# Joining the first two runs of decay levels in the last head of a gated-linear-attention layer

## The chip, the cores and the metric

The kernel runs on one core of a Trainium2 chip. The metric is device time in microseconds, taken as the median of several runs; the profile is that of one execution. Four compute engines work beside each other: TensorE (PE in the profile), VectorE (DVE), ScalarE (ACT) and GpSimd (POOL). SyncE (SP) issues the transfers between main memory and the core's working memory. TensorE writes only into accumulators (PSUM), which the other engines empty.

## The reference, cut to what matters

The program is a decoder of two layers over 1024 tokens with 1024 features. The first is gated linear attention with four heads, the second a dilated sliding-window attention with eight query heads. Each ends in an output projection, a residual and a layer norm. The change lies in the first layer. There, for every chunk, the reference computes an attention matrix whose products decay with the distance of the two tokens, separately for each of the 128 key features:

```python
b_all = jnp.cumsum(to_chunks(log_a), axis=3)
def step(state, inp):
    qc, kc, vc, bc = inp
    o_inter = jnp.einsum('bhcd,bhde->bhce', qc * jnp.exp(bc), state)
    diff = bc[:, :, :, None, :] - bc[:, :, None, :, :]
    decay = jnp.where(causal, jnp.exp(jnp.where(causal, diff, 0.0)), 0.0)
    att = jnp.einsum('bhid,bhjd,bhijd->bhij', qc, kc, decay)
    o_intra = jnp.einsum('bhij,bhje->bhie', att, vc)
    b_last = bc[:, :, -1:, :]
    new_state = jnp.exp(b_last[:, :, 0, :])[..., None] * state + \
        jnp.einsum('bhcd,bhce->bhde', kc * jnp.exp(b_last - bc), vc)
    return new_state, o_inter + o_intra
```

The head's output is normalised, multiplied by a gate, projected and added to the residual stream.

## The kernel before

**Decay by levels.** The kernel uses chunks of 128 tokens, eight of them. The factor `decay` depends on both tokens and on the feature, so the matrix is not one matmul. The function `levels` (from line 899) splits each 128 x 128 triangle into blocks: for L = 64, 32, 16, 8, 4, 2, 1 the block in which the query lies in the upper and the key in the lower half of a stretch of 2L tokens. Relative to the last token of the lower half both exponents have the right sign, so one tile X of 128 features x 1024 tokens holds the decayed queries in its upper halves and the decayed keys in its lower halves. X takes two subtractions, one exponential and two products (lines 908 to 916). The diagonal needs no decay; it is called L = 0 and uses q and k directly. There are three buffers for X, shared with a later tile `ke`.

**Runs.** The levels are walked in the order 0, 64, 32, 16, 8, 4, 2, 1 (line 904) and collected in the list `pair`. Once it is long enough (line 924), an accumulator tile `lv` of 128 x 512 is taken for every two levels, all their small matmuls (32 columns of the array each, 32 or 64 columns of data) are recorded as one group, and the results are copied out: L = 64 and 32 straight into the attention matrix `AT`, the others through a predicated copy into a compact tile `Dg`, which goes into `AT` behind the last run (line 961). There are two `lv` buffers. One level of 32 columns takes 32 matmuls (level 32 takes 16, level 64 takes 16 of 64 columns), each recorded as two instructions in the profile, as full-precision matmuls are.

In heads 0 to 2 the levels 0, 64, 32 and 16 form one run over both `lv` buffers, and 8 and 4, then 2 and 1, one run each. In head 3, the last, there are four runs of two levels each.

**What surrounds it.** `layer_a` ends with a loop over the heads (lines 1040 to 1050): gate, levels, `state_prep` (decayed queries and keys, with a transpose of the keys on TensorE), projections recorded behind them, and then `chunks` for each half of the tokens, which reads `AT` in its first matmul. For head 3 the projections are its own v and gate (lines 871 and 876), followed by `after`, which loads the stored outputs of the earlier heads for the output projection `out_ln`. The projections' wide matmuls are independent of the levels and fill TensorE while the other engines make the tiles X. Each wide product is done as three matmuls over split numbers (a high and a low part); the names `wh`, `wl`, `xh`, `xl`, `ogh`, `ogl` are these parts.

**Order of the work.** Nothing is issued as it is written. `Sched` records every operation, and `order` (from line 254) plans all of them from start to end with a table of costs: at each step it takes the operation that can begin earliest, and among equals the one recorded first, and for operations open to several engines (`vp`, `va`, `vap`) it also picks the engine. Every engine then executes its instructions in this order. A group is placed as a whole: all its inputs and all its new buffers must be at hand. The planner has no entry for the cost of changing from wide to narrow matmuls. Because all instructions are issued in one place, the profile shows the same line, 452, for nearly all of them; tiles' names tell them apart.

Of the kernel before, what the change touches and what calls it, by code (L numbers as in the profile page):

```python
# [18 lines left out]
GH = 4  # L19
# [578 lines left out]
def trunk(tc, xT, wP, wA, wA12, wAv3, w2, wO, wK, wV0, wV12, wB, wOB, par_d,  # L598
# [126 lines left out]
    def layer_a(t2, t1, after):  # L725
# [15 lines left out]
        def xtile(dt, name, shape=(128, T)):  # L741
            return t1.tile(list(shape), dt, name=name, tag="X", bufs=3)
# [156 lines left out]
        def levels(h):  # L899
            q, k, b = H[h]["q"], H[h]["k"], H[h]["b"]  # L900
            AT, Dg = ATs[h % 2], Dgs[h % 2]
            pair = []

            for li in (NLEV - 1, *range(NLEV - 1)):
                if li < len(LEVELS):
                    L = LEVELS[li]
                    n = T // (2 * L)
                    X = xtile(F32, "X")
                    view = lambda t: t.rearrange("p (n s l) -> p n s l", s=2, l=L)
                    bv, Xv = view(b), view(X)  # L910
                    ref = bv[:, :, 0, L - 1:L].to_broadcast([128, n, L])
                    S.vector.tensor_sub(Xv[:, :, 1, :], bv[:, :, 1, :], ref)
                    S.vp.tensor_sub(Xv[:, :, 0, :], ref, bv[:, :, 0, :])
                    S.scalar.activation(X, X, AF.Exp, scale=1.0 / 16.0)
                    S.vector.tensor_mul(Xv[:, :, 1, :], Xv[:, :, 1, :], view(q)[:, :, 1, :])
                    S.vp.tensor_mul(Xv[:, :, 0, :], Xv[:, :, 0, :], view(k)[:, :, 0, :])
                    lt, rt = X, X
                else:
                    L = 0
                    lt, rt = k, q  # L920


                pair.append((li, L, lt, rt))
                if len(pair) < (4 if h < GH - 1 and L in (0, 64, 32, 16) else 2):
                    continue
                pbs = [ps.tile([128, 2, 256], F32, name="lv", bufs=2) for _ in pair[::2]]
                with S.group():
                    for j, (_, L, lt, rt) in enumerate(pair):
                        pb, i = pbs[j // 2], j % 2
                        for c in range(NCH):  # L930
                            o = c * 128
                            if L == 64:

                                for s in (0, 32):
                                    d = c % 2 * 64 + s
                                    S.tensor.matmul(pb[d:d + 32, i, c // 2 * 64:c // 2 * 64 + 64],
                                                     lt[:, o + s:o + s + 32], rt[:, o + 64:o + 128],
                                                     start=True, stop=True)
                                continue
                            for s in (0, 64) if L == 32 else range(0, 128, 32):  # L940
                                e = s + 32 if L == 32 else s
                                S.tensor.matmul(pb[s:s + 32, i, c * 32:c * 32 + 32], lt[:, o + s:o + s + 32],
                                                 rt[:, o + e:o + e + 32], start=True, stop=True)
                for j, (lj, L, _, _) in enumerate(pair):
                    pb, i = pbs[j // 2], j % 2
                    if L == 64:
                        pl = pb[:, i].rearrange("p (c q) -> p c q", q=64)
                        AP = AT.rearrange("p (c two) i -> p two c i", two=2)
                        for x in range(2):
                            S.va.copy(AP[0:64, x, :, 64:128], pl[x * 64:x * 64 + 64])  # L950
                        continue
                    pl = pb[:, i].rearrange("p (c q) -> p c q", q=32)
                    if L == 32:
                        for s in (0, 64):
                            S.va.copy(AT[s:s + 32, :, s + 32:s + 64], pl[s:s + 32])
                    else:
                        S.vector.copy_predicated(
                            Dg, lmask[:, lj - 2:lj - 1, :].to_broadcast([128, NCH, 32]), pl)
                pair = []
            for s in range(0, 128, 32):  # L960
                S.va.copy(AT[s:s + 32, :, s:s + 32], Dg[s:s + 32])
# [78 lines left out]
        for h in range(GH):  # L1040
            gate(h)
            levels(h)
            state_prep(h)
            for f in ('qg', 'qVg', 'qg', 'vge')[h]:
                {"g": lambda: proj_g(h), "q": lambda: proj_qk(h + 1), "V": proj_v12, "v": lambda: proj_v(3), "e": lambda: after(0)}[f]()
            for g in range(2):
                chunks(h, g)
                finish(h, g)
                if h == GH - 1 and g == 0:
                    after(1)  # L1050
# [632 lines left out]
```

## Time and profile before

| | |
|---|---|
| median of 3 runs | 1153.51 us (1153.29 to 1153.53) |
| profiled execution, its own time | 1154.09 us |
| profiled execution, span from first to last instruction | 1152.2 us |
| granted TensorE clock, mean | 0.998 |
| TensorE busy | 1142.6 us (99%) |
| VectorE, ScalarE, GpSimd busy | 812.5, 457.7, 197.4 us |

The span is shorter than the execution's time, since that also holds what lies before the first and behind the last instruction. A row of the timeline gives start and length in microseconds, engine, line, operation, output and inputs by tile name, shape and count. Times count from the span's start. The four heads of the first layer lie at about 57 to 350 us, the first output projection behind them until about 440, the second layer until about 1100, and the last output projection up to the end.

### The profile page before, as it was taken

The numbers are of one execution on the slowest core, as the hardware profiler recorded it, in microseconds if no ns is written. First come the engines' busy times: TensorE is split into PE (matmuls) and PEld (weight loads), VectorE is DVE, ScalarE is ACT, GpSimd is POOL, SyncE is SP. The second block draws the span as 40 slices with busy tenths as digits, with TensorE's granted clock in tenths as the row PEclk, the third lists the DMA queues.
The fourth block names the chain that finished last, engine by engine and source line by source line (L and its number), as shares of the span: only waits on it lengthen the run. The fifth ranks groups of instructions, "written<-read, shape, count | busy, mean of one in ns | idle before, by whom it ended". The sixth has DMA issues, their size and how long they took to land.

```text
span 1152.2 us, 19793 instructions
## 1 busy us (share of the span) xinstructions
PE 1142.6 (99%) x7780; PEld 975.0 (85%) x7780; DVE 812.5 (71%) x1638; ACT 457.7 (40%) x964; POOL 197.4 (17%) x156
## 2 busy tenths in 40 slices
PE   9999999999999999999999999999999999999997
PEld 9888888889988888888888888888888888888886
DVE  6286862686966699765366868676778778768678
ACT  5355431645463335311214343434323433434342
POOL 1000100112011120221020314131221223213000
PEclk9999999999999999999999999999999999999999
DMA  8111222111144465543611211111151011134545
GB/s 271 56 39 38 74 75 92 38 57 54 59 171 139 139 203 160 173 143 104 210 40 36 56 38 57 38 40 54 38 166 39 20 39 38 39 93 129 188 141 183
DMA packets 93372, 108.39 MB, mean 94 GB/s; under 512 B 43648, under 2 KB 61952, under 8 KB 93280
## 3 DMA queue, kind: packets, MB, share of 16 engines
q1 hardware_dynamic: 93280, 107.13, 29.8%
q8 instruction: 61, 1.00, 0.4%
q14 instruction: 31, 0.25, 0.1%
HBM read 85.94 MB, written 21.17 MB: 93 GB/s over the span
## 4 chain that ended last, share of the span: by engine, by line
PE 94%; DVE 3%; DMA 1%; ACT 1%; issue 0%; SPq 0%; POOL 0%; DVEq 0%; ACTq 0%
PE acc L452 63%; PE lv L452 10%; PE po L452 9%; PE vac L452 7%; PE ms L452 4%; PE pro L452 2%; DVE rt L452 1%; DMA ogf<-ogB 1%; DVE wl L452 1%; DMA xf<-in_xT 0%; DVE x1l L452 0%; ACT wh L452 0%; ACT ogh L452 0%; DVE lnA L452 0%; SPq L452 0%
## 5 line engine op out<-in xcount | busy, mean ns | idle before, releaser
L452 PE MATMUL acc<-x1h,wh 128*128 128x512 f32 x608 | 252.2, 415 | 0.0
L452 PE MATMUL acc<-x1h,wl 128*128 128x512 f32 x608 | 237.6, 391 | 0.0
L452 PE MATMUL acc<-x1l,wh 128*128 128x512 f32 x608 | 237.0, 390 | 0.0
L452 ACT ACTIVATE wh<-wf 128x1024 fp32r<-128x1024 f32 (+2 forms) x104 | 108.1, 1040 | 267.0 <-PE acc L452 168.7
L452 POOL TENSOR_TENSOR wl<-wf,wh 128x1024 fp32r<-128x1024 f32 x41 | 98.3, 2397 | 530.4 <-ACT wh L452 352.3
L452 PEld LDWEIGHTS acc<-x1h,wl 128*128 128x128 f32 x608 | 114.1, 188 | 24.7
L452 PEld LDWEIGHTS acc<-x1l,wh 128*128 128x128 f32 x608 | 114.5, 188 | 21.3
L452 PEld LDWEIGHTS acc<-x1h,wh 128*128 128x128 f32 x608 | 114.4, 188 | 21.0
L452 ACT ACTIVATE P<-P,sts 128x128 f32<-128x128 f32 (+2 forms) x192 | 81.4, 425 | 121.7 <-DVE sts L452 121.4
L452 DVE TENSOR_TENSOR wl<-wf,wh 128x1024 fp32r<-128x1024 f32 (+2 forms) x64 | 80.9, 1265 | 57.3 <-ACT wh L452 45.3
L452 PE MATMUL acc<-xh,wh 128*128 128x512 f32 x256 | 101.7, 397 | 0.0
L452 PE MATMUL acc<-xh,wl 128*128 128x512 f32 x256 | 99.8, 390 | 0.0
L452 PE MATMUL acc<-xl,wh 128*128 128x512 f32 x256 | 99.8, 390 | 0.0
L452 DVE TENSOR_TENSOR t<-acc,cosT 128x512 f32<-128x512 f32 x60 | 41.3, 689 | 65.4 <-PE acc L452 65.3
L452 DVE TENSOR_TENSOR t<-acc,sinT 64x512 f32<-64x512 f32 x120 | 82.6, 688 | 1.6
L452 PE MATMUL lv<-K,Q 128*64 128x64 f32 (+2 forms) x512 | 69.4, 286 | 0.0
L452 DVE CUSTOM_DVE_ANT_0 P<-lv,bmask 128x256 f32<-128x256 f32 (+1 forms) x128 | 46.3, 379 | 29.3 <-PE lv L452 28.5
L452 DVE TENSOR_TENSOR Q<-t,t 128x512 f32<-128x512 f32 x44 | 61.7, 1402 | 1.2
L452 PEld LDWEIGHTS lv<-K,Q 128*128 128x128 f32 (+1 forms) x512 | 53.2, 163 | 10.0 <-issue 1.1
L452 PE MATMUL acc<-ogh,wh 128*128 128x512 f32 x152 | 60.3, 397 | 0.0
L452 PE MATMUL acc<-ogh,wl 128*128 128x512 f32 x152 | 59.2, 390 | 0.0
L452 PE MATMUL acc<-ogl,wh 128*128 128x512 f32 x152 | 59.2, 389 | 0.0
(250 smaller groups left out, 2230.1 us busy)
## 6 DMA issues: line engine op xcount, KB each, us to landing
wf<-in_wB SPq DMA_DIRECT2D x32, 512.0 KB
wf<-in_wA SPq DMA_DIRECT2D x24, 512.0 KB
wf<-in_wO SPq DMA_DIRECT2D x16, 512.0 KB
wf<-in_wOB SPq DMA_DIRECT2D x16, 512.0 KB
wf<-in_wV SPq DMA_DIRECT2D x12, 512.0 KB
res<-in_xT SPq DMA_DIRECT2D x16, 256.0 KB
x1d<-rt SPq DMA_DIRECT2D x16, 256.0 KB
out<-rt SPq DMA_DIRECT2D x16, 256.0 KB
```

Of the source, the lines that this page charges most:

```text
L452: getattr(handle[o.eng], meth)(*[conv(a) for a in args], **{k: conv(v) for k, v in kw.items()})
```

## The change

The condition that ends a run loses its exception for the last head, so that head 3 too collects the levels 0, 64, 32 and 16 into one run, which uses both `lv` buffers and needs three tiles X at once. Its runs of levels 8 and 4, and 2 and 1, stay. No instruction is added or removed; the planner works out the order anew for the whole program.

```diff
@@ -921,7 +921,7 @@
                 pair.append((li, L, lt, rt))
-                if len(pair) < (4 if h < GH - 1 and L in (0, 64, 32, 16) else 2):
+                if len(pair) < (4 if L in (0, 64, 32, 16) else 2):
                     continue
                 pbs = [ps.tile([128, 2, 256], F32, name="lv", bufs=2) for _ in pair[::2]]
```

## The prediction

> **What bounds the kernel now.** I read the page of the profile first, then the busy times by stage, then the order of instructions on each engine around the last head's levels.
>
> ```profile
> span 1152.2 us, 19793 instructions
> PE 1142.6 (99%) x7780; PEld 975.0 (85%) x7780; DVE 812.5 (71%) x1638; ACT 457.7 (40%) x964; POOL 197.4 (17%) x156
> PE 94%; DVE 3%; DMA 1%; ACT 1%; issue 0%; SPq 0%; POOL 0%; DVEq 0%; ACTq 0%
> ```
>
> TensorE (PE) is busy for 99% of the span, and 94% of the chain that ended last lies on it. Busy time alone does not prove the bound, because matmuls are pipelined and their ends are modelled. So I look at the stages (columns: length, then busy time and instructions of each engine, granted clock, DMA share, GB/s):
>
> ```profile
> 285.00:320.00 35.00, 35.00 (x651) 31.82 (x650) 32.01 (x50) 16.69 (x23) 3.79 (x3) 1.00 0.18 62
> 320.00:350.00 30.00, 30.00 (x167) 26.10 (x165) 19.05 (x34) 20.27 (x31) 6.20 (x4) 1.00 0.48 164
> 640.00:1100.00 460.00, 459.46 (x2610) 393.36 (x2609) 340.53 (x896) 175.43 (x534) 112.46 (x102) 1.00 0.25 69
> 1100.00:1152.00 52.00, 45.02 (x221) 37.91 (x219) 44.35 (x75) 20.19 (x34) 1.29 (x1) 0.96 0.45 149
> ```
>
> The changed work lies between 285 and 320. There PE has no idle time at the full clock, and VectorE (DVE) is the next engine at 32.01 of 35 us, so 91%. Only behind 1100 does PE stand still for long (52.00 - 45.02 = 6.98 us). The view of waits names no engine that PE's matmuls waited for in the changed stretch. What decides is therefore PE time, and the order in which DVE serves PE only if something becomes later than PE's other work can cover.
>
> **The two runs that are joined.** The order of PE's instructions in head 3 (start, length, output and inputs, tile, count) shows run one (k·q and level 64), then run two (levels 32 and 16):
>
> ```profile
> 290.47 0.63 PE L452 MATMUL ms<-sq,onesr 128*128 128x512 f32 x2
> 291.03 0.73 PE L452 MATMUL lv<-q,k 128*32 128x32 f32 x62
> ...
> 292.18 0.38 PE L452 MATMUL acc<-wh,xh 128*128 128x256 f32 x1
> 292.40 0.28 PE L452 MATMUL acc<-wl,xh 128*128 128x256 f32 x1
> 292.52 0.28 PE L452 MATMUL acc<-wh,xl 128*128 128x256 f32 x1
> ...
> 300.07 0.28 PE L452 MATMUL acc<-wh,xl 128*128 128x256 f32 x1
> 300.28 1.27 PE L452 MATMUL lv<-X 128*32 128x32 f32 x96
> 301.48 0.39 PE L452 MATMUL acc<-wh,xh 128*128 128x256 f32 x1
> 301.70 0.28 PE L452 MATMUL acc<-wl,xh 128*128 128x256 f32 x1
> ```
>
> In head 2 the same four levels already stand as one run:
>
> ```profile
> 239.42 0.39 PE L452 MATMUL acc<-xl,wh 128*128 128x512 f32 x1
> 239.65 0.39 PE L452 MATMUL acc<-xh,wl 128*128 128x512 f32 x1
> 239.97 0.73 PE L452 MATMUL lv<-q,k 128*32 128x32 f32 x62
> ...
> 240.55 1.67 PE L452 MATMUL lv<-X 128*32 128x64 f32 x126
> 242.14 0.50 PE L452 MATMUL acc<-xh,wh 128*128 128x512 f32 x1
> 242.48 0.40 PE L452 MATMUL acc<-xl,wh 128*128 128x512 f32 x1
> ```
>
> I charge a run with the time from the start of the last foreign matmul before it to the start of the second one behind it, less the steps which those foreign matmuls take anyway: 0.12 us for 256 columns (292.40 to 292.52) and 0.23 us for 512 (239.42 to 239.65). Run two: 301.70 - 300.07 = 1.63, less 2 x 0.12, makes 1.39 us. Run one: 292.40 - 290.47 = 1.93, less 2 x 0.23 and 0.12, makes 1.35 us. The joined run: 242.48 - 239.65 = 2.83, less 2 x 0.23, makes 2.37 us. **The saving is 1.35 + 1.39 - 2.37 = 0.37 us.** About 0.2 us of it is one switch from wide matmuls to narrow ones and back (for run two 301.70 - 300.07 = 1.63 less the 1.20 us from 300.28 to 301.48 and 0.24 leaves 0.19). The runs alone, without their switches, give the lower bound: (292.18 - 291.03) + (301.48 - 300.28) - (242.14 - 239.97) = 1.15 + 1.20 - 2.17 = 0.18 us. I take 0.37, since a switch delays all that stands behind it on a full PE, and keep 0.18 for the range.
>
> **The number of other instructions** does not change: the same 192 level matmuls, the same scratch tiles, two predicated copies and four plain copies out of the accumulators, the same two `lv` buffers. No DMA is added or moved, so nothing on the DMA queue is priced.
>
> **What becomes later.** The joined run needs the scratch tiles X of levels 64, 32 and 16 at once, which are all three that exist. Level 64's tile was free after run one (about 292) and served level 8 from 297.11 on; now it comes free after the joined run. The rows of DVE, ACT and PE that show what this moves:
>
> ```profile
> 297.11 0.68 DVE L452 TENSOR_TENSOR X<-b 128x512 f32<-128x512 f32 x1
> 298.91 0.68 DVE L452 TENSOR_TENSOR X<-b 128x512 f32<-128x512 f32 x1
> 299.63 1.06 ACT L452 ACTIVATE X<-X 128x1024 f32<-128x1024 f32 x1 [0.65 <-DVE X L452]
> 302.00 0.45 DVE L452 COPY_PREDICATED Dg<-lmask,lv 128x256 f32<-128x256 uint8 x1 [1.07 <-ACT AT L452]
> 321.13 1.70 ACT L452 ACTIVATE AT<-Dg 32x256 f32<-32x256 f32 x4
> 325.96 0.69 DVE L452 COPY sg<-acc 128x512 f32<-128x512 f32 x1 [4.86 <-PE acc L452]
> 331.20 0.61 PE L452 MATMUL po<-AT,v 128*128 128x128 f32 x4
> ```
>
> Level 8's two subtractions (0.68 each) and its exponential (1.06) move behind the joined run, together with one predicated copy (0.45): 2 x 0.68 + 1.06 + 0.45 = 2.87 us of work in a chain that had them done early. DVE's idle 1.07 us ahead of 302.00 takes some back, so I expect the third run 1 to 3 us later than 309.81. The other heads give the same from outside (chain of waits; start, length, what):
>
> ```profile
> 135.36 2.18 PE lv L452 x159
> 147.96 1.29 PE lv L452 x98
> 155.62 1.29 PE lv L452 x98
> 240.03 2.18 PE lv L452 x159
> 252.63 1.29 PE lv L452 x98
> 261.68 1.29 PE lv L452 x98
> 309.81 1.30 PE lv L452 x98
> 318.13 1.29 PE lv L452 x98
> ```
>
> From joined run to third run they need 12.60 us (240.03 to 252.63, 135.36 to 147.96), and to the last run 9.05 or 7.66 more. With a joined run at 300.3 this puts the third run at 312.9 and the last at 320.6 to 322.0, so 2 to 4 us later than 318.13.
>
> **I cost this delay at nothing.** What is late next is the attention matrix AT. It is complete at 321.13 + 1.70 = 322.83, but its first reader is the matmul at 331.20, behind the gate projection, whose whole work lies ahead of it on PE in any case. That is a cover of 8.37 us against 2 to 4, and DVE has 4.86 us idle ahead of 325.96 to catch up. If the cover were gone, PE would wait one microsecond per microsecond. From below, an earlier run could gain nothing either, since that PE work stays in front. So the bounds of this term are 0 and, with the whole 2.87 us exposed, +2.9.
>
> **The sum**: the profiled execution took 1154.09 us (span 1152.2, and 1.9 around it). 1154.09 - 0.37 = 1153.72. That execution lies 0.58 above the median of the timed runs, 1153.51, so the forecast for the median is 1153.51 - 0.37 = **1153.1 us**, with 1152.9 to 1156.0 as the bounds of the two terms (the upper with 0.18 saved and 2.9 exposed). What a measurement can tell from no change is about 0.2%, 2.3 us, so this is "no change".
>
> **The rivals.** *The order further on changes for the worse.* The order of all later work is worked out by a planner from start to end, so a shifted DVE queue near 300 can alter it. The price is extra switches on PE at 0.2 us. To be over 0.2% slower it takes (2.3 + 0.37) / 0.2 = 13 of them. With two more in each of the eight query heads of layer B: 1153.1 + 16 x 0.2 = **1156.3**. For it speaks that DVE is 91% busy where the shift occurs. Against it, PE's work up to 331.20 is the same set either way, so the queues can fall back into the old order behind it; and layer B runs in a strict rhythm, which does not look sensitive to how it was entered:
>
> ```profile
> 652.13 2.07 PE acc L452 x9
> 713.09 2.07 PE acc L452 x9
> 774.05 2.07 PE acc L452 x9
> ```
>
> These are the same place in three heads in a row, 60.96 us apart each time. Chance 0.09.
>
> *The levels end too late.* Place: the PE queue at 331.20. It decides from a delay of 8.37 us on; to cost over 0.2% net it needs 8.37 + 2.67 = 11.0 us, and with 12 it gives 1153.1 + 3.6 = **1156.7**. For it: three tiles are held at once, on an engine at 91%. Against: the other heads' spacing allows 4. Chance 0.03. [...]
>
> *The order further on changes for the better.* With two switches fewer in each of eight heads, or half of the 6.98 us won at the end: 1153.1 - 3.2 = **1149.9** or 1149.6. For it: the last stage is the only one where PE stands still, and its order follows from what came before. Against: no part of the change touches it. Chance 0.08.
>
> **How the numbers follow.** The likeliest case, no change within 0.2%, has 0.80, and 1153.1 is its time. Faster by over 0.2% has 0.08, slower 0.12 (0.09 and 0.03). The range is 1151.2 to 1156.3: below it reaches to the edge of 0.2%, above to the first slower case, beyond the exposed delay of 1156.0.
>
> **What would show it.** In the profile after: one run of 192 level matmuls in head 3 at 298 to 301, with about 2.2 us from its start to the next wide matmul; level 8's subtractions behind it; the third run at 311 to 313, the last at 319 to 322; the first matmul on AT within 0.5 us of 331, with no wait on PE ahead of it; layer B with 60.96 us between heads and the same stage times. I am wrong if PE idles before 331, if the stages of layer B change their length by more than 1 us in all, or if the time moves by over 2.3 us.

## The result, and the profile after

The changed kernel took 1157.86 us in the median (six executions, 1156.17 to 1159.83), the kernel before on the same chip 1153.52 (six, 1153.29 to 1155.06). The ratio is 1.0031 with a 95% interval of 1.0021 to 1.0041: **slower by 0.31%**, where 1153.1 us had been forecast. The profiled execution of the changed kernel took 1156.17 us, with these lines on its page:

```profile
span 1154.4 us, 19793 instructions
...
PE 1143.0 (99%) x7780; PEld 974.7 (84%) x7780; DVE 816.2 (71%) x1640; ACT 456.5 (40%) x963; POOL 194.3 (17%) x155
...
q8 instruction: 61, 1.00, 0.4%
...
PE 96%; DVE 3%; issue 1%; ACT 0%; DVEq 0%
```

The counts of PE are those of before; one instruction has gone from ACT and one from POOL to DVE. The busy times by stage, columns as before:

```profile
285.00:320.00 35.00, 33.07 (x604) 30.17 (x606) 29.24 (x48) 15.44 (x23) 2.80 (x2) 1.00 0.18 62
640.00:1100.00 460.00, 460.00 (x2614) 393.98 (x2613) 342.65 (x906) 174.61 (x534) 111.03 (x102) 1.00 0.24 68
1100.00:1154.00 54.00, 47.04 (x229) 39.22 (x227) 44.76 (x76) 21.05 (x34) 1.29 (x1) 0.98 0.44 153
331.00:362.00 31.00, 30.64 (x163) 25.65 (x162) 25.59 (x37) 19.79 (x29) 9.73 (x6) 1.00 0.42 149
```

In the changed stretch PE now stands still for 35.00 - 33.07 = 1.93 us, where it had no idle time. Layer B (640 to 1100) and the end (6.96 us idle against 6.98) are as they were. From 331 to 362 PE executes 163 matmuls where the kernel before executes 169:

```profile
331.00:362.00 31.00, 31.00 (x169) 26.86 (x168) 24.50 (x39) 19.94 (x28) 10.30 (x6) 1.00 0.35 118
```

I matched the matmuls of the two profiled executions by their position in the order of starts (both have 7780) and took the difference of their starts, after less before. It is -0.67 us up to 285, before anything differs; two executions of one same kernel differ there by 0.3 us too (before_mid96 and before_mid96_b, below). It becomes +1.07 by 303, +1.19 by 330 and +2.44 by 362, and stays so to 1050. **So the change costs 1.74 us between 285 and 303, 1.25 us between 331 and 362, and 0.12 us between these two places.** At the end 0.4 us comes back. The two losses have different causes. These sizes are those of the profiled execution, the fastest of the six; the other five have no trace.

### The profile page after: what moved, and what is told of

Its sections match the earlier page's. It is cut to its first block, busy times and chain, and to the rows that moved or that the text cites. A ratio compares the mean times of both kernels' runs of the same rounds, so it can differ in the third digit from the quotient of the medians.

```text
span 1154.4 us, 19793 instructions
## 1 busy us (share of the span) xinstructions
PE 1143.0 (99%) x7780; PEld 974.7 (84%) x7780; DVE 816.2 (71%) x1640; ACT 456.5 (40%) x963; POOL 194.3 (17%) x155
## 4 chain that ended last, share of the span: by engine, by line
PE 96%; DVE 3%; issue 1%; ACT 0%; DVEq 0%
PE acc L452 64%; PE lv L452 10%; PE po L452 9%; PE vac L452 7%; PE ms L452 4%; PE pro L452 2%; DVE rt L452 1%; DVE wl L452 1%; DVE x1l L452 0%; DVE lnA L452 0%; ACT wh L452 0%; DVE oT L452 0%; ACT sq L452 0%; DVE sum L452 0%; DVE ogl L452 0%
## 5 line engine op out<-in xcount | busy, mean ns | idle before, releaser
L452 POOL TENSOR_TENSOR wl<-wf,wh 128x1024 fp32r<-128x1024 f32 x40 | 95.8, 2396 | 513.1 <-ACT wh L452 355.3
```

What stands on the lines that cost most here:

```text
L452: getattr(handle[o.eng], meth)(*[conv(a) for a in args], **{k: conv(v) for k, v in kw.items()})
```

## First loss: PE runs out of instructions

The order of PE's instructions in head 3, after (a bracket names the idle time ahead of a row and what ended it; "issue" is time in which nothing that the profile shows was waited for):

```profile
298.03 0.28 PE L452 MATMUL acc<-wh,xl 128*128 128x256 f32 x1
298.24 0.73 PE L452 MATMUL lv<-q,k 128*32 128x32 f32 x62
...
298.82 1.56 PE L452 MATMUL lv<-X 128*32 128x64 f32 x115
302.32 0.32 PE L452 MATMUL lv<-X 128*32 128x32 f32 x11 [1.93 <-issue]
302.56 0.38 PE L452 MATMUL acc<-wh,xh 128*128 128x256 f32 x1
302.79 0.28 PE L452 MATMUL acc<-wl,xh 128*128 128x256 f32 x1
```

The joined run starts at 298.24, within the forecast 298 to 301, and would have taken 2.2 us. But 11 matmuls before its end PE stands still for 1.93 us. No input was missing: the last 64 matmuls of the run are those of level 16, all of them read the same tile X, and 53 of them had been executed. The waits of PE list it as the longest, and no engine as its cause:

```profile
PE lv L452 <- issue: 1.9, 1, 1.9
PE pro L452 <- DVE Dg L452: 1.2, 1, 1.2
```

What was late shows on a DMA queue (q8) whose kind the page calls "instruction". Over the whole span it has 61 packets and 1.00 MB, hence 16.4 KB a packet. PE has 7780 matmuls and 7780 weight loads, 15,560 rows, and 15,560 / 61 makes 255 rows a packet. In the trace of the changed kernel the first of the 61 starts at 14.47 us, behind 174 rows of PE and its sequencer, and the last at 1132.79, behind 15,516, so one starts for every 255.7 rows. From 298 to 303 the view of transfers has one such packet (packets, MB, share of 16 engines); by the trace it starts at 299.6, in the middle of the joined run, and takes 1.35 us:

```profile
q8 instruction: 1, 0.02, 1.7%
```

A run of four levels is 192 matmuls and 192 weight loads, 384 instructions, and takes them in about 2.1 us. Among wide matmuls PE takes two instructions per 0.23 us (512 columns) or 0.12 us (256 columns, as ahead of this run), so 9 or 17 a microsecond; in the run it takes some 180. In the kernels of this text PE goes dry nine times inside a joined run, and each time at the same row modulo 256 of its instructions (matmuls, weight loads and 127 rows of its sequencer, counted from the start). From these positions and the packets' starts I worked out a picture. It is an estimate, since no trace shows a request or what PE still has: the instructions come in blocks of 256, the next block is asked for when a certain row of the present one is reached, and PE then has some 320 instructions left. In this run the request would fall on row 44, so at about 298.24 + 44 / 180 = 298.5; PE stops 364 rows in, 320 behind the request, and goes on at 302.32, 3.8 us behind it. Let p be the number of rows from a run's start to the next such row (modulo 256). The joined runs of heads 0, 1 and 2 have p = 98, 164 and 103 in the kernel before, and none stands still. The new one in head 3 has p = 44: the request is early in the run, and the 340 instructions of the run behind it are more than the 320 that PE has left by the estimate. Among wide matmuls no trace here has a stand-still by "issue"; in this run of 384 narrow instructions the row above shows 1.93 us.

### Moving the runs against the blocks

The rival to this picture was that the new order, not the supply, makes the stand-still. Two kernels put 16 narrow matmuls, each 32 x 32, at the very start, into both the kernel before and the changed one, and two put 50 there. That displaces all later instructions against the blocks. The matmuls' results are used by nothing.

```diff
+            for _ in range(16):
+                S.tensor.matmul(accs[7][0:32, 0:32], Dgs[0][:, 0, :], Dgs[0][:, 1, :], start=True, stop=True)
```

> The kernel before with the same 16 matmuls at the start. Theory 1: heads 0 and 2 have joined runs here too, so the unchanged kernel becomes slower by two gaps of about 2 us or more: 1156.5 to 1163. Theory 2: 1153.5 plus at most 0.5 us.

> The changed kernel with 16 such matmuls at the start (64 instructions). Theory 1: the fetch in head 3 now falls ahead of the joined run, but those of heads 0 and 2 fall about 34 and 39 instructions behind their runs' starts, so PE stands still in heads 0 and 2 for about 2 us each and not in head 3: 2 us or more over the changed kernel, 1157 to 1164, with two gaps in the trace. Theory 2: 1156 to 1160 and no gap in heads 0 and 2.

> The kernel before with the same 50 matmuls at the start. It measures what these cost by themselves. Both theories: 1153.5 plus 0 to 1.5 us, since PE waits for the first data there in any case.

> The changed kernel with 50 matmuls of 32x32 added at the very start (200 recorded instructions on PE), the order of all else unchanged; their results are never read. Theory 1, instruction supply: a block of 256 PE instructions is fetched while the one before it runs, and the joined run of head 3 (384 instructions in about 2.1 us) uses up its block before the next has landed, because a fetch is asked for only about 44 instructions after the run's start. With the stream moved by 200 instructions no joined run meets a fetch in its first 80 instructions, so the 1.93 us without work in head 3 goes, and the time is 1153.1 plus at most 1.5 us for the added matmuls: 1152.8 to 1154.6. Theory 2, order: the new order of the other engines' work costs the time; the order is unchanged here, so the time stays near 1157.9 (1156 to 1160).

The kernel before on this chip took 1154.70 us. Measured: before_shift64 1159.03 (ratio 1.0048, 1.0034 to 1.0061), after_shift64 1163.54 (1.0082, 1.0069 to 1.0095), before_shift200 1156.89 (1.0024, 1.0014 to 1.0034), after_shift200 1158.44 (1.0036, 1.0023 to 1.0049). PE's waits of before_shift64, a kernel without the change:

```profile
PE lv L452 <- issue: 4.5, 2, 2.3
```

of after_shift64:

```profile
PE lv L452 <- issue: 5.3, 3, 2.0
```

and of after_shift200:

```profile
PE pro L452 <- DVE Dg L452: 1.2, 1, 1.2
PE ms L452 <- DVE S L452: 0.3, 1, 0.3
```

By moving instructions alone, the stand-still appears in the old kernel in the joined runs of heads 0 and 2 (p = 34 and 39), and it goes from the changed kernel's head 3 (after_shift200). That it depends on the place of the run against the blocks is shown. The exact rule isn't: after_shift64 stood still in head 3 as well, where p = 236 and I had expected nothing, while all joined runs with a p from 98 to 220 that occurred went through. The place of that stand-still fits the picture: a request row lies 256 - 236 = 20 rows ahead of the run, and PE stops 300 rows into it, again 320 behind a request. That it stops at all fits too: matmuls of 256 columns stand ahead of this run, so the 20 rows are only 1.3 us, and PE runs dry 3.15 us behind the request, where in the other eight cases it goes on 3.5 to 4.3 us behind it. Only the size doesn't fit: PE goes on 4.96 us behind the request, and stands still for 1.81 us instead of 0.3 to 1.2.

The time of after_shift200 missed the first theory: 1152.8 to 1154.6 was expected, 1158.44 came, inside the range of the second. Its stand-still is gone all the same. Part of the miss is the 50 matmuls, whose control before_shift200 takes 2.19 us more than the kernel before and not at most 1.5. They are 100 rows of PE, 0.032 us apart at a granted clock of 1.00, and take 3.16 us; 48 such rows at 270 us in after_mid96 (below) have the same 0.032. The other 1.55 us, by which after_shift200 lies over its control, are not the supply's: the second loss below is in this kernel too.

### Shorter runs

The other test takes the length instead of the place. It gives every head two levels a run, so no run has more than 256 instructions, at the same displacement.

```diff
-                if len(pair) < (4 if h < GH - 1 and L in (0, 64, 32, 16) else 2):
+                if len(pair) < 2:
```

> The kernel before with two levels a run in every head, so that no run has more than 256 instructions, and 16 narrow matmuls at the very start, the displacement at which before_shift64 stood still in heads 0 and 2 (2.0 and 2.5 us) and took 1159.0 us. Theory (a run of 384 instructions outruns the supply, one of at most 256 doesn't): no stand-still in any run of levels; three joinings undone cost 3 x 0.4 us and the narrow matmuls some 1 us: 1155.5 to 1157.5 where the kernel before takes 1154.4. Rival (the displacement itself brings the stand-still, whatever the run's length): gaps of about 2 us in some runs again, 1159 or more.

1157.33 us (ratio 1.0026, 1.0015 to 1.0036, the kernel before at 1154.20), inside the expected range and some 1.2 us closer to its kernel before than before_shift64 was to its own (3.1 against 4.3 us). No run stands still: among PE's waits there is none by "issue". So it takes the long run and the bad place together. The 3.1 us hold the three joinings undone (3 x 0.37 us by the prediction's price) and the 16 matmuls (32 rows, 1.3 us in its trace); 0.7 us of them stay unexplained.

### A halved clock behind the stand-still

In the profiled execution of the changed kernel the clock stays at 1.00 through 300 to 310. In others it does not. The busy times of after_old2 (below), which has the same stand-still:

```profile
300.00:305.00 5.00, 2.85 (x133) 2.71 (x122) 2.35 (x5) 2.44 (x5) 0.00 (x0) 0.90 0.02 7
305.00:310.00 5.00, 5.00 (x33) 4.87 (x32) 3.97 (x7) 2.07 (x4) 0.00 (x0) 0.76 0.00 0
```

and PE's order there:

```profile
303.51 0.32 PE L479 MATMUL lv<-X 128*32 128x32 f32 x11 [2.15 <-issue]
303.76 0.42 PE L479 MATMUL acc<-wh,xh 128*128 128x256 f32 x1
303.98 0.41 PE L479 MATMUL acc<-wl,xh 128*128 128x256 f32 x1
...
307.18 0.37 PE L479 MATMUL acc<-wl,xh 128*128 128x256 f32 x1
307.39 0.28 PE L479 MATMUL acc<-wh,xl 128*128 128x256 f32 x1
307.51 0.28 PE L479 MATMUL acc<-wh,xh 128*128 128x256 f32 x1
```

For 3.6 us matmuls of 256 columns follow each other at 0.21 us instead of 0.12; 16 of them make 16 x 0.093 = 1.5 us. The clock says the same: (0.10 + 0.24) x 5 us / 0.5 = 3.4 us at half speed. (That the stretch has half speed is an estimate from the step, 0.21 against 0.12, and from the one granted value below 1.00 in the traces of the two kernels: 0.50 behind 1151.5 in the changed kernel, behind 1147.7 in the kernel before, where no matmul stands.) In after_shift64 matmuls of 512 columns follow each other at 0.43 us instead of 0.23 from 79.6 to 83.0. Of the nine stand-stills in the traces, four have such a stretch of 3.4 us behind them: those of after_old2 and after_pool (below; 0.71 from 305 to 310), that of head 0 in after_shift64 (0.95 from 75 to 80, 0.71 from 80 to 85) and that of head 2 in before_shift64 (0.98 from 245 to 250, 0.68 from 250 to 255). They lasted 2.0 to 2.2 us. The other five, of 1.5 to 2.3 us, have a full clock behind them, those in the profiled executions of the changed kernel and of after_oldorder among them. That this explains why the changed kernel spreads over 3.7 us (1156.17 to 1159.83), with its profiled execution the fastest, fits the numbers: the mean granted clock of the six is 0.999 in the fastest, 0.998 in the next three and 0.997 in the two slowest, where 3.4 us at half speed take 0.0015 off. But the kernel before has 0.998 and 0.999 too, and the other executions have no trace, so it is argued and not shown. In these nine the length of the stand-still alone does not decide it: behind 2.0 to 2.2 us the stretch followed in four cases, and behind 2.28 us (before_shift64, head 0) the clock stayed at 1.00. What decides it is not shown.

## Second loss: the order behind the levels

The planner worked out a new order behind the joined run, and the loss from 331 to 362 comes from it. The first thing that it moves is `ke`, the decayed keys from which the chunks' state is made. DVE's and ACT's rows before:

```profile
315.27 1.06 ACT L452 ACTIVATE ke<-ke 128x1024 f32<-128x1024 f32 x1 [2.03 <-DVE ke L452]
...
316.36 1.23 DVE L452 TENSOR_TENSOR ke<-ke,k 128x1024 f32<-128x1024 f32 x1
...
319.35 1.09 PE L452 MATMUL ms<-ident,ke 128*128 128x128 f32 x8
...
320.51 0.80 SPq L452 DMA_DIRECT2D ogf<-ogA  x2
...
333.16 0.48 DVE L452 SCALAR_TENSOR_TENSOR S<-S,dec,ms 128x256 f32<-128x256 f32 x1 [0.46 <-PE ms L452]
```

and after (SP's queue is the row SPq):

```profile
319.03 1.06 ACT L452 ACTIVATE wh<-wf 128x1024 fp32r<-128x1024 f32 x1 [4.04 <-PE acc L452]
320.00 1.04 ACT L452 ACTIVATE ke<-ke 128x1024 f32<-128x1024 f32 x1
...
322.08 1.22 DVE L452 TENSOR_TENSOR ke<-ke,k 128x1024 f32<-128x1024 f32 x1
...
324.00 1.03 PE L452 MATMUL ms<-ident,ke 128*128 128x128 f32 x8
...
325.10 6.70 SPq L452 DMA_DIRECT2D ogf<-ogA  x12
...
331.55 1.29 ACT L452 ACTIVATE ogh<-ogf 128x512 fp32r<-128x512 f32 x2 [0.85 <-DMA ogf<-ogA]
...
333.82 1.51 DVE L452 TENSOR_TENSOR wl<-wf,wh 128x1024 fp32r<-128x1024 f32 x1
...
335.85 1.05 DVE L452 SCALAR_TENSOR_TENSOR S<-S,dec,ms 128x256 f32<-128x256 f32 x2
```

On ACT the exponential of `ke` now stands behind a weight conversion that waits 4.04 us for PE, and on DVE its product stands behind a weight split and two copies. PE turns `ke` at 324.00 instead of 319.35. `ke` lies in the pool of the tiles X, and the loads `ogf` take their buffers from a pool that opens when that one is closed (line 609). So SP asks for the first `ogf` 0.07 us behind the end of the turning, in either kernel: 325.10 instead of 320.51. ACT then waits for these loads, DVE for ACT, and the state S comes late. On DVE a weight split of 1.51 us also stands ahead of the second update of S: 335.85 instead of 333.16, of which 1.2 us are what PE is behind by then. Before, GpSimd made this split:

```profile
332.31 2.38 POOL L452 TENSOR_TENSOR wl<-wf,wh 128x1024 fp32r<-128x1024 f32 x1 [20.17 <-PE ms L452]
```

### Without the stand-still

To see this loss alone, 24 narrow matmuls are put ahead of head 3's gate when the order has been worked out already, so it stays the planner's. They move the joined run to p = 204. The kernel before with the same addition is the control.

```diff
+                if h == GH - 1 and half == 0:
+                    S.ops[-1].pad = (24, z[0:32, 0:32], ident[:, 0:32])
...
             for o in done:
...
+                if getattr(o, "pad", None):
+                    n, z, x = o.pad
+                    for _ in range(n):
+                        nc.tensor.matmul(conv(z), conv(x), conv(x), start=True, stop=True)
```

> The changed kernel with 24 matmuls of 32x32 (96 recorded instructions) put on PE ahead of head 3's gate matmul, about 25 us ahead of its joined run and behind the runs of heads 0 to 2; the order of all else is unchanged, and their results are overwritten. Theory 1a, supply alone: the joined run no longer meets a fetch in its first part, the stand-still goes, and the time falls to 1153.1 plus 0.5 to 1 us for the added matmuls: 1153.5 to 1154.2. Theory 1b, supply and order: the stand-still goes, but the loss of about 2 us between 335 and 360 stays: 1155.2 to 1156.2. Theory 2, order alone: about 1158.

> The kernel before with the same 24 matmuls in the same place, as a measure of what they cost: 1153.5 plus 0.5 to 1 us under every theory, no stand-still, since no run of head 3 has more than 256 instructions.

The kernel before took 1154.42 us on this chip, before_mid96 1155.87 (ratio 1.0012, 1.0003 to 1.0021) and after_mid96 1156.89 (1.0025, 1.0015 to 1.0034). So without the stand-still, 1.0 us of loss remains: the fastest execution of after_mid96 (1156.53) is slower than ten of the eleven of before_mid96. Theory 1b, supply and order, had this pattern, but its time of 1155.2 to 1156.2 was missed, since the 24 matmuls cost 1.45 us and not 0.5 to 1.

Two kernels were to give the weight split back to GpSimd, but I marked the wrong piece (the output projection's second instead of its third), so the split between the updates of S stayed on VectorE:

```diff
-        out_ln(0, hs(half), lambda et: load_w(wO[et]), lambda et: xT[et * 128:et * 128 + 128, :], emit_a)
+        out_ln(0, hs(half), lambda et: load_w(wO[et], half == 0 and et == 1), lambda et: xT[et * 128:et * 128 + 128, :], emit_a)
```

> As after_mid96, and one instruction more is changed: the low part of the second weight piece of the first output projection, which the new order puts on VectorE between two state updates of head 3, runs on GpSimd, where the order before had it. Theory 1b: the state update comes about 2 us earlier, the chunks of head 3 and the output projection keep pace, and the time is 0 to 0.5 us below before_mid96: 1153.5 to 1154.5. Theory 1a: same as after_mid96.

> The changed kernel with that one instruction on GpSimd and no matmuls added. Theory 1b: the stand-still of about 2 us in head 3, and what follows it, stays, the loss behind 335 us goes: 1.5 to 2 us below the changed kernel, 1155 to 1157. Theory 1a: same as the changed kernel, 1156 to 1160.

after_mid96_pool took 1157.37 us (1.0027) and after_pool, without the 24 matmuls, 1159.58 (1.0042). Both came out as expected for a split without effect, but since another piece was moved they say nothing about that split; after_pool gave the halved clock above.

### Part of the old order

The next kernels put back the order of before, by a list of record numbers and engines that replaces part of the planned order: first from the third run of head 3 on.

```diff
         done = self.order()
+        by = {o.seq: o for o in done[1333:1516]}
+        for i, x in enumerate(OLD):
+            o = by[int(x[:-1])]
+            o.eng = {"P": "PE", "A": "ACT", "D": "DVE", "G": "POOL", "S": "SP"}[x[-1]]
+            done[1333 + i] = o
```

The third of them leaves the new order and gives the right weight split to GpSimd (`et == 2` in the diff above).

> The changed kernel with 24 narrow matmuls ahead of head 3's gate (as in after_mid96, so that the joined run doesn't stand still) and, from the third run of head 3 to 360 us, with every instruction in the order and on the engine that the kernel before has: the split of the output weight goes back to GpSimd and no longer stands ahead of the state updates on VectorE. Theory (two causes, instruction supply and the new order): neither is left, only the joining's saving of some 0.4 us, so 0.2 to 0.6 us under before_mid96, 1155.2 to 1155.9 where the kernel before takes 1154.4; TensorE's matmuls from 329 to 360 keep their distance to those of before_mid96 within 0.4 us. Rival (the later levels themselves cost it, since the cover is not there): 1.0 us over before_mid96 as after_mid96 was, 1156.9.

> The changed kernel in the order of before from the third run of head 3 on, without the narrow matmuls: the joined run lies as in the changed kernel against the blocks of instructions. Theory (two causes): the stand-still of 1.9 to 2.4 us in the joined run of head 3 is there, the loss between 335 and 360 is not; 1.5 to 2.0 us over the kernel before (1155.9 to 1156.4), up to 1158 in executions in which the clock is halved behind the stand-still. Rival (the order is all, the stand-still is hidden by later waits): 0.4 us under the kernel before.

> after_mid96 with one instruction on another engine: the low part of the output weight that stands between head 3's state updates on VectorE is made by GpSimd, as in the kernel before; the order of everything else stays the new one. If this split is what delays the state updates: they come 1.0 to 1.2 us earlier and the time is 0.2 to 1.0 us under after_mid96 (1155.9 to 1156.7 where after_mid96 takes 1156.9). If it is the rest of the order: 1156.9 as after_mid96.

after_mid96_oldorder took 1156.61 us (1.0021, 1.0012 to 1.0030), after_oldorder 1158.55 (1.0034, 1.0021 to 1.0047), where the kernel before took 1154.20. Both theories' first numbers were missed: the loss had not gone. The reason is on SP and PE: what makes `ke` stands ahead of the place from which the order was put back, and in after_mid96_oldorder it still came late. SP's first load there:

```profile
324.89 7.27 SPq L478 DMA_DIRECT2D ogf<-ogA  x12
```

PE's wait for S:

```profile
PE po L478 <- DVE S L478: 1.2, 1, 1.2
```

and its busy time:

```profile
331.00:362.00 31.00, 29.76 (x162) 25.65 (x162) 24.46 (x38) 21.49 (x31) 9.74 (x6) 1.00 0.44 148
```

PE stands still for 31.00 - 29.76 = 1.24 us. after_mid96_wlpool took 1158.80 us (ratio 1.0035, 1.0023 to 1.0047), over both expected times and no better than after_mid96. Its profiled execution took 1265.75 us at a clock of 0.948, so its times can't be compared with the others. Its order on DVE can: while GpSimd made the weight split (2.36 us from 363.57), another split, of `ogf`, took 2.78 us on DVE (from 363.71) where it takes 0.69 elsewhere, and the update of S began 3.53 us behind S's copy, against 2.44 in after_mid96. So in this execution S gained nothing by moving the split. Why DVE was slow there, and what the split alone costs, is left open.

### The old order from the joined run on

> The changed kernel with the 24 narrow matmuls (no stand-still), and every engine's and SP's order from the joined run on that of the kernel before, so that of the change only the joining itself is left: ke is made and turned right behind the third run, as before, and SP asks for the gated outputs at once. Theory (the late turn of ke): TensorE turns ke at 320 to 321, SP issues the first load of ogf at 321 to 322 and not at 325, ScalarE doesn't wait for these loads at 331, TensorE doesn't wait 1.2 us for the state S; 0 to 0.5 us under before_mid96_b, a ratio to the kernel before of 1.0007 to 1.0013. Rival (the later levels alone delay the states): 0.7 us and more over before_mid96_b.

> As after_mid96_old2, but only up to the turn of ke and the loads of ogf: from there on the new order stays, with the output weight's split on VectorE ahead of the state updates. Theory (the late turn of ke makes the loss): at most 0.4 us over after_mid96_old2. Rival (the split between the state updates makes it too): 0.6 to 1.2 us over after_mid96_old2.

> The kernel before with the 24 narrow matmuls, as the control on the same chip: 1.2 to 1.6 us over the kernel before, as before_mid96 was.

> The changed kernel without the narrow matmuls, with the order of before from the joined run on. Theory (two causes, of which the stand-still alone is left): a gap of 1.7 to 2.1 us in the joined run, ke turned at 321 to 322, and 1.0 to 1.8 us over the kernel before, more in executions with a halved clock behind the gap; so some 1.0 us less than the changed kernel's 1157.9. Rival (the stand-still costs nothing, since it is made up before 331): 0.4 us under the kernel before.

The edit is that of above, with a list that starts at position 1242, right behind the joined run. The kernel before took 1154.15 us on this chip, before_mid96_b 1155.58 (ratio 1.0012, 1.0003 to 1.0021), after_mid96_old2 1156.25 (1.0019, 1.0010 to 1.0028), after_mid96_ke 1157.43 (1.0030, 1.0018 to 1.0041), after_old2 1155.45 (1.0015, 1.0006 to 1.0023). The medians are only just apart, so the matched matmuls have to say more. Change of the difference to before_mid96_b by stage, in us; for the two kernels without the 24 matmuls, to the kernel before:

| kernel | 285-303 | 303-318 | 318-331 | 331-362 | sum |
|---|---|---|---|---|---|
| before_mid96 (same kernel) | 0.00 | +0.02 | 0.00 | -0.20 | -0.18 |
| after_mid96 (new order) | -0.37 | -0.02 | +0.12 | +1.90 | +1.63 |
| after_mid96_oldorder (`ke` late, rest old) | -0.37 | -0.04 | +0.09 | +1.31 | +0.99 |
| after_mid96_ke (`ke` early, rest new) | -0.36 | +0.71 | 0.00 | +1.06 | +1.41 |
| after_mid96_old2 (all old) | -0.37 | +0.70 | +0.01 | -0.16 | +0.18 |
| the changed kernel | +1.74 | +0.02 | +0.10 | +1.25 | +3.11 |
| after_old2 | +3.20 | +0.28 | -0.01 | 0.00 | +3.47 |

The busy times from 331 to 362 agree, for before_mid96_b:

```profile
331.00:362.00 31.00, 31.00 (x168) 26.77 (x167) 24.46 (x38) 21.31 (x31) 9.86 (x6) 1.00 0.40 138
```

after_mid96_ke:

```profile
331.00:362.00 31.00, 30.62 (x164) 25.64 (x163) 24.75 (x36) 20.12 (x28) 8.44 (x5) 1.00 0.37 128
```

and after_mid96_old2, with the stage ahead of it:

```profile
303.00:318.00 15.00, 14.67 (x200) 12.51 (x201) 13.44 (x22) 8.16 (x11) 2.12 (x1) 1.00 0.21 72
331.00:362.00 31.00, 31.00 (x168) 26.85 (x167) 24.46 (x38) 22.01 (x31) 10.14 (x6) 1.00 0.40 139
```

Of the same kernel the third run, cut in two by a wait, and SP's first load:

```profile
312.43 0.75 PE L483 MATMUL lv<-X 128*32 128x32 f32 x64 [0.30 <-DVE X L483]
...
322.59 0.80 SPq L483 DMA_DIRECT2D ogf<-ogA  x2
```

Four things follow. The order put back whole takes the loss from 331 to 362 away (-0.16 us), and SP's load starts at 322.59 instead of 325. Both halves of the new order cost something, the late `ke` 1.31 us and the order behind it 1.06, while together they cost 1.90. These are single executions, and the whole new order costs between 1.25 us (the changed kernel) and 2.06 (after_shift200 against before_shift200) in this stage, so that the two overlap isn't shown. The median of after_mid96_ke is 1.2 us over that of after_mid96_old2, as the rival written down for it had said, though the intervals of their ratios overlap. With the old order the third run waits for its tile X and 0.70 us is lost at 303 to 318 instead, where the planner's order loses 0.02: in these kernels the work that the joining displaces on DVE shows either there or behind 331. What is left of the change then is +0.18 us, against -0.18 between two executions of the control itself, so nothing measurable. The median of after_mid96_old2 lies 0.67 us over before_mid96_b and not 0 to 0.5 as expected; the intervals of the two ratios overlap, and in its profiled execution 0.8 arises behind 1100, in a wait at the end that some executions of other kernels have too.

after_old2 has the stand-still alone: its profiled execution, the slowest of eleven, loses 3.47 us up to 318, by the stand-still and the slowed stretch, which lies on both sides of 303, and nothing more behind 318. Its median, 1155.45 us, is 1.3 us over the kernel before, as expected. The changed kernel's was 4.3 over its own, on another chip, so the gain is larger than the 1.0 us expected. No version beat the kernel before.

## Why the prediction was wrong, point by point

- **The saving of 0.37 us** was right where the run goes through: four kernels without a stand-still show -0.36 to -0.37 at 285 to 303.
- **"I take 0.37"** assumed that 192 narrow matmuls take in head 3 the 2.37 us that they take in head 2. This step failed. The same run at another place among the blocks of instructions takes some 2 us more (a stand-still of 1.93 us in the profiled execution, 1.5 to 2.3 over all kernels), and in some executions another 1.5 at a halved clock. The sum had no term for it and no rival named it; the row of head 2 from which the price came had p = 103 by luck of its place.
- **"No DMA is added or moved, so nothing on the DMA queue is priced"** failed. SP's loads of the gated outputs started 4.6 us later, because their buffers depend on `ke`, and `ke` had slipped behind weight work on ACT and DVE (1.2 of the 4.6 us are PE's own delay by then).
- **"I cost this delay at nothing"** looked at one reader only. The third run came at 311.49 and the last at 319.15, as forecast:

```profile
311.49 1.36 PE L452 MATMUL lv<-X 128*32 128x32 f32 x128
...
319.15 1.36 PE L452 MATMUL lv<-X 128*32 128x32 f32 x128
...
332.39 0.61 PE L452 MATMUL po<-AT,v 128*128 128x128 f32 x4
```

  AT's first reader moved by 332.39 - 331.20 = 1.19 us, which is what PE was behind by then, with no wait ahead of it: the cover for AT held. But AT was not what is late next. The chain from `ke` through the loads and splits to S had no such cover, and its price, 1.3 to 1.9 us, lies inside the bound of 2.9 that was worked out for AT.
- **The rivals.** "The order further on changes for the worse" was the right side and had 0.09. Its place was wrong: not switches in layer B, which keeps its 60.96 us between heads (rows of the chain), but 331 to 362. "The levels end too late" did not occur: PE had no wait ahead of AT's first reader at 332.39, and none for the `lv` buffers appears among its waits.

```profile
654.58 2.07 PE acc L452 x9
...
715.54 2.07 PE acc L452 x9
...
776.50 2.07 PE acc L452 x9
```

- **The range** ended at 1156.3 and the median was 1157.86. The supply alone (after_old2, 1.3 us over the kernel before) or the order alone (after_mid96, 1.0 us over its control) would have stayed inside it; both together did not. These two medians make 2.3 of the 4.3 us that the changed kernel lost, and its profiled execution lost 2.65; what the rest is in the slower executions is not shown. The candidates seen are the halved clock and a larger second loss (2.78 us from 331 to 362 in after_pool). By the signs that the prediction named, PE idling before 331 and a time that moves by over 2.3 us, it was wrong as well.

## What to carry to other kernels

A run of small matmuls can stand still for want of instructions, as runs of 384 did here nine times for 1.5 to 2.3 us, and whether it does depends on how many instructions stand ahead of it in the whole program (64 more rows at the start of the old kernel brought it to two runs); keep dense runs to 256 instructions, as none of that length or shorter stood still here, or look for idle time by "issue" in their middle after every edit, also far away ones. When something is delayed in a planned order, ask of every tile that dies with it what waits for its space, transfers above all, and not only who reads its result. The gain of 0.37 us from merging work on the busiest engine was worth nothing here, where the second engine, at 91%, had to move its own work for it.

## What was not expected of the hardware

- PE went dry for 1.5 to 2.3 us inside runs of 384 narrow instructions in about 2.1 us, never inside runs of 256 instructions or fewer, and only at some places against the blocks of 256.
- After a stand-still of about 2 us the granted clock fell in four of nine cases (0.68 to 0.76 over five microseconds, by the estimate above half speed for 3.4 us) and stayed at 1.00 in the others.
- Fifty matmuls of 32 x 32 into one and the same place took 3.16 us in after_shift200, 32 ns for each of their 100 rows in the profile at a granted clock of 1.00 (the 48 rows in after_mid96 alike), where the joined run takes about 11 ns a row. Why is not shown.
